# A fixed table of numbers instead of a greedy list sets the order of 1874 operations (input projection, convolution and attention) and of the 235 after them

## The chip, the cores and the metric

The kernel runs on one core of one Trainium2 chip. The time of a run is the device time of one launch in microseconds (us). Before the change three runs took 1118.74 us in the median (1118.23, 1118.74 and 1120.79). Lower is better. A core has a matmul engine (PE, TensorE, with its weight loads in a lane of their own, PEld), a vector engine (DVE), a scalar engine (ACT), a general engine (POOL, GpSimd) and a sync engine (SP) that here only issues DMAs. Each works through its own instructions strictly in the order in which they were written.

## The reference

One layer of a decoder: 1024 tokens, width 1024, float32.

```python
h = rms_norm(x, norm1_g)
q, k, v, glu_a, glu_b = split(h @ w_in)          # five times 512 columns
q, k = rms_norm(q per head), rms_norm(k per head) # 8 heads of 64
# stick-breaking attention, strictly causal, in blocks of 128 queries:
z = q @ k.T / 8;  beta = sigmoid(z)
A[t, s] = beta[t, s] * prod(1 - beta[t, j] for s < j < t);  attn = A @ v
c = glu_a * sigmoid(glu_b)
c = silu(layer_norm(causal_depthwise_conv(c, width 31)))
x = x + concat([attn, c]) @ w_out
h = rms_norm(x, norm2_g);  gate, val = split(h @ w_up)   # two times 2816 columns
x = x + (silu(causal_depthwise_conv(gate, width 3)) * val) @ w_down
```

## The kernel before

**Precision.** Every large product is made in three matmuls of a 512-column tile (`mm3`, L325 to L327): each operand is split into a high half, which the PE takes at its fast rate, and the low half that is left over, and high times high, low times high and high times low are added up in one PSUM bank. So each operand costs a rounding copy (the "high", mostly on ACT) and a subtraction (the "low", mostly on DVE, which reads what ACT wrote).

**Stages, in order of time.** (1) 0 to 40 us: the eight 128-token tiles of x are loaded (`load_x`, L422), squared on ACT (L431), given 1/rms on POOL (L316, L317), scaled on DVE (L435), turned by the PE (`hT`, L444) and split (L448 ACT, L449 DVE). The weights come in pieces (L475), are split (L479 ACT, L483 DVE), and the first products for v begin. The small parameters come as one operation of ten DMAs (`params`, L842 to L877, DMAs L850 to L855). (2) 40 to 236 us: the projections on the PE, and beside them the convolution on DVE, ACT and POOL. (3) 236 to 429.5 us: attention, head by head, with the last part of the convolution and the convolution's half of the output projection (`op`, L1353 its sum) put in between. (4) 429.5 to about 500 us: the attention's half of the output projection (`opa`, L1484 its sum), the second norm, and the turning of its result (`h2T`). (5) to 905 us the wide FFN products, (6) to the end the last product (`dn`, L1848).

**Attention.** For one head and one block of 128 queries (`tb`): the PE makes the scores in one or two pieces (`z`, L1172 and L1173), ACT makes 1 - beta of them (`nb`, L1180), DVE runs the products along the row as a scan (L1194), POOL or ACT takes one off the result (`less`, L1199 on POOL, L1201 on ACT). Two such blocks make a group g (0 to 3). The PE turns the group's weights (`wT`, L1221: `wT7_3_2` is head 7, group 3, source pair 2), they are split (high: ACT L1232, or DVE; L1230 for the triangle on the diagonal; low: DVE L1242, diagonal L1237), and the PE multiplies them with v into `po` (L1249). Two groups share one `po` bank, which ACT (L1277) and DVE (L1280) then fetch into `attn`. Keys and queries of a head are split and turned before (L1076 to L1136). DVE thus stands twice in the chain of each block, in the scan and in the low half.

**The end of attention.** Four pieces of 128 rows of w_out's attention half (`rawo`) are loaded into two places (L1387), split into `hio` (ACT, L1391) and `loo` (DVE, L1396), and `opa` takes them in the order of rows 0, 1, 3, 2.

**What sets the order.** All the work up to the end of attention is not emitted as it is written but collected in a `Plan`: 1874 operations, each with its engine or its alternatives (`{"ACT": 600, "DVE": 690}`, a cost in ns), the operations it comes after, the buffer places that it takes, and a key, which is about its due time. `Plan.run` (L124 to L204) is a list scheduler: at each step it looks at the operations that are ready and whose key is at most `HORIZON` above the lowest key open, works out for each the engine on which it would end first, and emits the one that could start first, where an operation that stands next by its key is given 150 ns (`PATIENCE`) of advantage. A second plan of 235 operations does the same for stage 4 and the first operands of stage 5. Afterwards `in_order` (L401) chains the emitted instructions of PE, DVE, ACT and POOL, so that each engine takes them in the order of emission. Stages 5 and 6 lie outside the plans.

## Time and profile before

| | |
|---|---|
| three runs | 1118.23, 1118.74, 1120.79 us |
| profiled execution | its time is its span, 1118.1 us |
| TensorE clock, mean share granted | 1.00 from 40 us on |
| PE | 1094.5 us busy, 98% of the span |
| DVE, ACT, POOL | 884.7, 618.6, 546.6 us |
| bytes moved | 118.5 MB, mean 106 GB/s |

A row of a timeline gives start, duration, engine, line of the code, operation and "out<-in" by the names of the tiles, then in brackets the idle time just before it and what ended that. A row of waits gives the waiting engine and line, the one waited for, the total in us, how often, and the longest. A row of a table of windows gives the stretch, its length, then busy time and instructions of PE, PEld, DVE, ACT and POOL, the granted clock, the DMAs' busy share and GB/s. A row of groups gives line, engine, operation, tiles, shapes and count, then busy us and mean ns of one, then the idle time in front of them. For PE a matmul's row lasts longer than the distance to the next one (0.39 us and 0.23 us for 512 columns), since matmuls are pipelined.

### The profile page before, as it was taken

Reading aid. Unit: us, or ns where it says so; the run is one execution under the profiler, and the core shown is the slowest. Engines: PE = TensorE matmul, PEld = TensorE weight load, DVE = VectorE, ACT = ScalarE, POOL = GpSimd, SP = SyncE. Lnnn points to the kernel's source line nnn. Section 1 sums busy time; section 2 is a strip of 40 time slices with the busy share of each in tenths; the row PEclk is TensorE's granted clock in tenths of the full one; section 3 lists DMA queues with packets and bytes.
Section 4 is the critical chain, followed back from the end, with each engine's and each line's share of the span. In section 5 each row is a group of like instructions: output and inputs, shape, how many; then the busy total and the mean of one; then the engine's idle time right before and its main releaser. Section 6 shows DMA issues by size and latency. Waiting matters only on the chain.

```text
span 1118.1 us, 14908 instructions
## 1 busy us (share of the span) xinstructions
PE 1094.5 (98%) x5255; PEld 906.2 (81%) x5255; DVE 884.7 (79%) x1188; ACT 618.6 (55%) x1137; POOL 546.6 (49%) x485
## 2 busy tenths in 40 slices
PE   8999999989999999989999999999999999999998
PEld 5888888768888887868888888888888888888887
DVE  6498899579998886889886777777777668787895
ACT  7344567787887674654443433333333378776760
POOL 3165587566344432656332233223323189887770
PEclk9999999999999999999999999999999999999999
DMA  8110500333933224442232231312222482303304
GB/s 286 57 39 8 143 20 24 95 128 88 282 121 113 58 76 151 154 147 76 94 93 96 73 97 59 107 62 97 73 95 76 141 323 83 143 14 146 151 2 150
DMA packets 110234, 118.54 MB, mean 106 GB/s; under 512 B 21105, under 2 KB 89936, under 8 KB 110158
## 3 DMA queue, kind: packets, MB, share of 16 engines
q1 hardware_dynamic: 110014, 117.05, 32.1%
q8 instruction: 42, 0.69, 0.3%
q10 hardware_dynamic: 144, 0.52, 0.1%
q14 instruction: 34, 0.28, 0.1%
HBM read 82.95 MB, written 28.31 MB: 100 GB/s over the span
## 4 chain that ended last, share of the span: by engine, by line
PE 77%; DVE 9%; POOL 4%; ACT 4%; DMA 2%; issue 2%; SPq 0%; POOLq 0%; DVEq 0%; ACTq 0%
PE dn L1848 19%; PE u_S L326 7%; PE u_S L327 7%; PE u_S L325 7%; PE u L327 5%; PE u L326 5%; PE u L325 5%; POOL attn L725 3%; PE po L1249 2%; PE wT L1221 2%; DVE nb L1194 2%; PE opa L325 1%; PE opa L327 1%; PE opa L326 1%; PE z L1172 1%
## 5 line engine op out<-in xcount | busy, mean ns | idle before, releaser
L1848 PE MATMUL dn<-wd,wd 128*128 128x512 f32 x768 | 181.5, 389 | 0.0
L1848 PEld LDWEIGHTS dn<-wd,wd 128*128 128x128 f32 x768 | 144.0, 188 | 30.1 <-DVE c L1851 0.2
L326 PE MATMUL u_S<-bT,aS 128*128 128x512 f32 x264 | 102.8, 389 | 0.8 <-DVE bT L1523 0.8
L327 PE MATMUL u_S<-bT,aS 128*128 128x512 f32 x264 | 102.7, 389 | 0.0
L325 PE MATMUL u_S<-bT,aS 128*128 128x512 f32 x264 | 102.5, 390 | 0.0
L1851 DVE TENSOR_TENSOR c<-dn,c 128x512 f32<-128x512 f32 x120 | 81.0, 684 | 23.9 <-PE dn L1848 23.7
L321 ACT CAST aS<-rawu 128x512 fp32r<-128x512 f32 x63 | 38.9, 621 | 96.2 <-PE u_S L327 66.9
L1753 ACT CAST wd<-rawd 128x512 fp32r<-128x512 f32 x128 | 72.6, 618 | 32.7 <-DMA rawd<-in_w_down_dram 10.8
L1194 DVE TENSOR_TENSOR_SCAN nb<-nb,one 128x128 f32<-128x128 f32 (+4 forms) x64 | 84.8, 1340 | 2.9 <-ACT nb L1180 2.7
L1595 POOL TENSOR_TENSOR s<-rawu 128x512 f32<-128x512 f32 x21 | 29.7, 1415 | 101.7 <-DMA rawu<-in_w_up_dram 92.5
L1752 ACT COPY whole<-rawd 128x512 f32<-128x512 f32 x110 | 63.4, 585 | 24.3 <-DVE wd L1754 11.2
L1754 DVE TENSOR_TENSOR wd<-whole,wd 128x512 fp32r<-128x512 f32 x90 | 59.9, 683 | 16.5 <-ACT wd L1753 9.4
L1601 POOL TENSOR_TENSOR rawu<-rawu 128x512 f32<-128x512 f32 x21 | 29.0, 1381 | 81.2 <-DVE a L322 81.2
L1697 DVE SCALAR_TENSOR_TENSOR y<-gv,cols_a,y 128x1023 f32<-128x1023 f32 (+1 forms) x44 | 59.6, 1355 | 10.2 <-ACT y L1695 10.2
L321 ACT CAST a<-rawu 128x512 fp32r<-128x512 f32 x63 | 39.0, 621 | 49.9 <-PE u_S L327 31.1
L325 PE MATMUL u<-b,a 128*128 128x512 f32 x168 | 65.5, 390 | 0.0
L327 PE MATMUL u<-b,a 128*128 128x512 f32 x168 | 65.5, 390 | 0.0
L326 PE MATMUL u<-b,a 128*128 128x512 f32 x168 | 65.4, 389 | 0.0
L326 PEld LDWEIGHTS u_S<-bT,aS 128*128 128x128 f32 x264 | 49.6, 188 | 11.4 <-POOL raws L1560 1.2
L325 PEld LDWEIGHTS u_S<-bT,aS 128*128 128x128 f32 x264 | 49.5, 188 | 10.7 <-ACT bT L1522 0.4
L327 PEld LDWEIGHTS u_S<-bT,aS 128*128 128x128 f32 x264 | 49.6, 188 | 10.3
L322 DVE TENSOR_TENSOR a<-rawu,a 128x512 fp32r<-128x512 f32 x63 | 47.0, 748 | 13.2 <-ACT a L321 13.2
(343 smaller groups left out, 3213.6 us busy)
## 6 DMA issues: line engine op xcount, KB each, us to landing
rawu<-in_w_up_dram SPq DMA_DIRECT2D x44, 512.0 KB
act_d<-y SPq DMA_DIRECT2D x22, 512.0 KB
rawd<-act_d SPq DMA_DIRECT2D x22, 512.0 KB
rawd<-in_w_down_dram SPq DMA_DIRECT2D x22, 512.0 KB
raw_qk<-in_w_in_dram SPq DMA_DIRECT2D x16, 256.0 KB
rawo<-in_w_out_dram SPq DMA_DIRECT2D x8, 512.0 KB
m<-conv_d SPq DMA_DIRECT2D x16, 256.0 KB
xt<-in_x_dram SPq DMA_DIRECT2D x8, 512.0 KB
```

The source lines that it names most:

```text
L321: nc.scalar.copy(hi, src)
L322: lo_engine.tensor_tensor(lo, src, f32(hi), op=ALU.subtract)
L325: nc.tensor.matmul(ps, a_hi, b_hi, start=first, stop=False)
L326: nc.tensor.matmul(ps, a_hi, b_lo, start=False, stop=False)
L327: nc.tensor.matmul(ps, a_lo, b_hi, start=False, stop=last)
L1194: nc.vector.tensor_tensor_scan(rev, rev, ones_of[0][:, :w], 0.0, op0=ALU.mult, op1=ALU.max)
L1697: nc.vector.scalar_tensor_tensor(y[:, j:], g[:, :S - j], par("fw", (KF - 1 - j) * NF + f), y[:, j:], op0=ALU.mult, op1=ALU.add)
L1752: nc.scalar.copy(whole, src)
L1753: nc.scalar.copy(t[:, 0], src)
L1754: lo_engine.tensor_tensor(t[:, 1], whole, f32(t[:, 0]), op=ALU.subtract)
L1848: nc.tensor.matmul(ps, a[:, tok], b, start=first and m == 0, stop=last and m == 2, skip_group_check=True)
L1851: nc.vector.tensor_tensor(sums[c][s], ps, sums[c][s], op=ALU.add)
```

## The change

`Plan.run` no longer chooses. It is given a list of numbers and emits the operations in that order: 1874 numbers for the first plan and 235 for the second. `HORIZON` and `PATIENCE` go. What it still works out as it walks through the list is on which of its alternative engines an operation runs and which buffer place it gets; that goes by costs, and these are changed: hand-over times by engine, a time for PE's results to come out, a time for PE to start again after a pause, and some thirty operations' own costs (most by less than a third). Two dependencies are added: the keys' split of every head but the first also waits for the last use of the weights whose room it takes, and the first `po` product of an odd group waits for the last of the even one. No operation is added or taken away, and nothing changes outside the two plans.

```diff
-    HAND_OVER, POOL_HAND_OVER = 60, 130
+    HAND_OVER = {"ACT": 36, "DVE": 36, "POOL": 86, "PE": 56, "SP": 30}
+    OVER = {"PE": 0, "ACT": 104, "DVE": 82, "POOL": 36, "SP": 0}
+    PE_DRAIN, PE_RESTART = 163, 100
...
-    def run(self, busy):
+    def run(self, order):
...
-            for op in ready:
-                if op.key > horizon:
-                    continue
...
-                rank = (max(start - PATIENCE, at[e]), op.key) if op.key <= main[low].key + 1 else (start, op.key)
+        for op in (self.ops[n] for n in order):
+            slots = self.slots_for(op.takes)
...
+                    r = max(r, o.end + (0 if o.engine == e == "PE" else Plan.HAND_OVER[e] + (Plan.PE_DRAIN if o.engine == "PE" else 0)))
+                start = max(r, at[e])
+                if e == "PE" and start > at[e] + 30:
+                    cost += Plan.PE_RESTART
...
-        k2 = split_op("k", staged, 0, base - (2.6 if h else EARLY), ready, khl)
+        k2 = split_op("k", staged, 0, base - (2.6 if h else EARLY), ready + (second_used if h else []), khl)
...
-                b = add({"POOL": 100 + 1.03 * w, "ACT": 160 + 0.86 * w}, less, i - AHEAD_SCAN + 0.3 * u, [a])
+                b = add({"POOL": 192 + 0.84 * w, "ACT": 296 + 0.84 * w}, less, i - AHEAD_SCAN + 0.3 * u, [a])
...
-                last = add("PE", 480, products, k, [c] + v2 + ([last] if last else []))
+                last = add("PE", 480, products, k, [c] + v2 + ([last] if last else [prev_last] if g % 2 else []))
...
-    plan.run({})
+    plan.run(ORDERS[0])
...
-    plan.run({})
+    plan.run(ORDERS[1])
```

The first places of the two lists:

```diff
+ORDERS = [[int(n) for n in numbers.split()] for numbers in ("""
+0 13 32 1 25 33 41 34 35 42 2 4 43 95 15 38 7 47 36 37 26 5 3 44 39 104 45 105 48 59 60 22 24 6 46 106 49 113 68 114
```

Lines past L260 have numbers higher by 60 in the changed kernel (L1194 becomes L1254); the text keeps the numbers of before.

**DVE at the start of attention.** Before the change, these rows stand on DVE from the first scan (L1194) on; `conv_lo` (L820) is the last of the convolution, `nb0_0` to `nb0_3` are rows of head 0, and `rest<-qT` (L1136) is the low half of its queries.

```order
L1194 SCALAR_TENSOR_TENSOR nb0_0_2204<-nb0_0_2204,one_1898 128x128
L1194 SCALAR_TENSOR_TENSOR nb0_2_2215<-nb0_2_2215,one_1898 128x384
L820 TENSOR_TENSOR conv_lo1_0_2230<-conv_out0_812,conv_hi1_0_2229 128x512
L1136 SCALAR_TENSOR_TENSOR rest_2170<-qT0_1_2239,qgain_130,keys_2148 128x512
L820 TENSOR_TENSOR conv_lo1_0_2230<-conv_out1_1087,conv_hi1_0_2229 128x512
L1194 SCALAR_TENSOR_TENSOR nb0_1_2249<-nb0_1_2249,one_1898 128x256
L1194 SCALAR_TENSOR_TENSOR nb0_3_2266<-nb0_3_2266,one_1898 128x512
L1230 CAST diagonal_0_1752<-wT0_0_0_2275 128x384
```

After the change, the same place on DVE:

```order
L1196 SCALAR_TENSOR_TENSOR rest_2198<-qT0_0_2187,qgain_130,keys_2154 128x512
L880 TENSOR_TENSOR conv_lo1_0_2223<-conv_out0_878,conv_hi1_0_2222 128x512
L1254 SCALAR_TENSOR_TENSOR nb0_2_2230<-nb0_2_2230,one_2184 128x384
L1196 SCALAR_TENSOR_TENSOR rest_2198<-qT0_1_2236,qgain_130,keys_2154 128x512
L1254 SCALAR_TENSOR_TENSOR nb0_0_2227<-nb0_0_2227,one_2184 128x128
L1159 CAST keys_2154<-kT1_0_2217 128x512
L1254 SCALAR_TENSOR_TENSOR nb0_1_2269<-nb0_1_2269,one_2184 128x256
L1196 SCALAR_TENSOR_TENSOR rest_2198<-qT1_0_2263,qgain_130,keys_2154 128x512
L880 TENSOR_TENSOR conv_lo1_0_2223<-conv_out1_1176,conv_hi1_0_2222 128x512
L1290 CAST diagonal_0_1825<-wT0_0_0_2301 128x384
```

The queries' low halves, those of head 1 among them, and a copy of head 1's keys have come in between the first scans, so that a scan stands after other work that does not need it.

**DVE at the end of attention.** Before, from the low half of `wT7_3_0` to the last fetch of `po` (`attn`, L1280):

```order
L1396 TENSOR_TENSOR loo2_4300<-rawo_4165,hio2_4299 128x1024
L1242 TENSOR_TENSOR tl_2344<-wT7_3_0_4330,rest_2170 128x512
L1242 TENSOR_TENSOR tl_2344<-wT7_3_1_4336,rest_2170 128x512
L1232 CAST rest_2170<-wT7_3_2_4342 128x512
L1242 TENSOR_TENSOR tl_2344<-wT7_3_2_4342,rest_2170 128x512
L1237 TENSOR_TENSOR diagonal_1_2985<-wT7_3_3_4349,diagonal_1_2985 128x384
L1396 TENSOR_TENSOR loo3_4376<-rawo_4165,hio3_4375 128x1024
L1280 TENSOR_TENSOR attn_110<-po7_2_4269,attn_110 64x512
```

After, the same place on DVE:

```order
L1302 TENSOR_TENSOR tl_2407<-wT7_3_0_4325,rest_2198 128x512
L1302 TENSOR_TENSOR tl_2407<-wT7_3_1_4315,rest_2198 128x512
L1456 TENSOR_TENSOR loo0_4341<-rawo_3825,hio0_4340 128x1024
L1302 TENSOR_TENSOR tl_2407<-wT7_3_2_4355,rest_2198 128x512
L1297 TENSOR_TENSOR diagonal_1_3067<-wT7_3_3_4343,diagonal_1_3067 128x384
L1456 TENSOR_TENSOR loo3_4373<-rawo_3825,hio3_4372 128x1024
L1340 TENSOR_TENSOR attn_110<-po7_2_4276,attn_110 64x512
L1456 TENSOR_TENSOR loo1_4396<-rawo_3825,hio1_4395 128x1024
```

The low half of w_out's second piece (`loo1`), which `opa` takes second, now stands behind the fetch of the last `po`, and on ACT its high half (`hio1`) stands behind that fetch in the same way; before, both pieces 0 and 1 were made well ahead.

**SP at the opening.** Before, the tiles of x are all issued ahead of the parameters (`param_rows`):

```order
L422 DMA x_q0_139<-in_x_dram 128x1024
L422 DMA x_qk1_140<-in_x_dram 128x1024 x4
L475 DMA raw_glu_b0_246<-in_w_in_dram 128x8x128
L850 DMA param_rows_272<-in_conv_dw_b_dram 4x128
L850 DMA param_rows_272<-in_conv_ln_g_dram 4x128
```

After, the same queue:

```order
L535 DMA raw_v_2_237<-in_w_in_dram 128x2x256 x2
L910 DMA param_rows_247<-in_conv_dw_b_dram 4x128
L910 DMA param_rows_247<-in_conv_ln_g_dram 4x128
L910 DMA param_rows_247<-in_conv_ln_b_dram 4x128
L910 DMA param_rows_247<-in_ffn_dw_b_dram 22x128
L913 DMA param_rows_247<-in_q_norm_g_dram 1x64 x2
L913 DMA param_rows_247<-in_k_norm_g_dram 1x64 x2
L914 DMA param_rows_247<-in_ffn_dw_w_dram 66x128
L915 DMA param_rows_247<-in_conv_dw_w_dram 124x128
L482 DMA x_qk1_140<-in_x_dram 128x1024 x3
L482 DMA x_q0_139<-in_x_dram 128x1024
```

The ten parameter loads now stand ahead of four of the eight tiles of x and of the last piece of v's weights.

128 lines of the change are left out of this document (50 added, 78 removed), and 80 rows, old and new, of the table ORDERS.

## The prediction

> **What bounds the kernel now.** I read the page's first line, then a table of windows cut at the stages (the columns: stretch, length, busy us of PE, PEld, DVE, ACT and POOL with their instructions, clock, DMA share, GB/s).
>
> ```profile
> span 1118.1 us, 14908 instructions
> ```
>
> ```profile
> 0.00:40.00 40.00, 34.58 (x164) 25.44 (x164) 26.91 (x38) 25.36 (x44) 13.04 (x24) 0.96 0.69 226
> 40.00:235.70 195.70, 194.74 (x893) 159.78 (x891) 156.68 (x219) 111.97 (x253) 117.25 (x114) 1.00 0.20 59
> 235.70:317.30 81.60, 75.66 (x475) 64.62 (x473) 76.06 (x98) 66.67 (x131) 42.19 (x45) 1.00 0.55 165
> 317.30:429.50 112.20, 108.36 (x704) 94.10 (x704) 97.80 (x118) 82.75 (x157) 43.57 (x46) 1.00 0.28 89
> 429.50:500.00 70.50, 66.80 (x321) 54.04 (x320) 56.19 (x87) 40.77 (x80) 36.48 (x41) 1.00 0.48 159
> 500.00:904.90 404.90, 404.90 (x1788) 335.31 (x1787) 302.31 (x366) 154.81 (x223) 139.66 (x96) 1.00 0.30 97
> ```
>
> PE is the bound. An order can win only the time in which PE waits inside the planned part, and none after 500 us, where PE is never idle and the plans no longer rule. Idle PE (length less the first busy figure) is 5.42, 0.96, 5.94, 3.84 and 3.70 us in the first five rows.
>
> That is not yet all that is lost, as a matmul's row overlaps the next:
>
> ```profile
> 452.97 0.39 PE L327 MATMUL opa<-hio,m 128*128 128x512 f32 x1
> 453.89 0.47 PE L325 MATMUL opa<-hio,m 128*128 128x512 f32 x1 [0.54 <-DVE x L1484]
> 454.20 0.40 PE L326 MATMUL opa<-loo,m 128*128 128x512 f32 x1
> ```
>
> Matmuls of this form start 0.23 us apart when nothing is late. Here the starts lie 0.92 apart, so 0.69 is lost where the bracket shows 0.54, and the next start comes 0.08 late again (0.31 for 0.23). So I took in the trace every distance between two starts of PE, less the usual one of its form, and added them up: 6.2 us up to 40, 2.3 to 235.7, 10.7 to 317.3 (26 stops), 8.8 to 429.5 (35 stops), 5.5 to 500. The first and the last of these 61 stops in attention:
>
> ```profile
> 241.58 0.45 PE L1172 MATMUL z<-keys 128*128 128x384 f32 x1 [1.05 <-ACT nb L1180]
> ...
> 428.57 0.38 PE L1249 MATMUL po<-tl,rest 128*128 128x256 f32 x1 [0.41 <-DVE tl L1242]
> ```
>
> What PE waits for most in attention, then what DVE itself waits for in the first stretch, and in the second (total, times, longest):
>
> ```profile
> PE z L1172 <- ACT nb L1180: 3.4, 6, 1.1
> PE po L1249 <- DVE tl L1242: 1.4, 3, 0.8
> PE wT L1221 <- DVE tl L1242: 1.4, 2, 0.8
> ```
>
> ```profile
> DVE nb L1194 <- ACT nb L1180: 2.6, 4, 1.1
> DVE rest L1136 <- ACT keys L1133: 1.4, 1, 1.4
> ```
>
> ```profile
> DVE tl L1242 <- ACT rest L1232: 6.3, 7, 2.1
> DVE diagonal L1237 <- ACT diagonal L1230: 2.5, 4, 1.2
> ```
>
> Two different pictures. In the first stretch DVE is busy 76.06 us of 81.60, more than PE: both are near full, and DVE's 5.5 idle us are lost to its order. In the second DVE has 14.4 us to spare, PE 3.8: there the stops are a matter of distance, of how much PE work stands between what PE makes and what it needs back.
>
> **The change part by part.**
>
> *PE's work* stays the same, instruction for instruction; only its order differs. The stages after 500 us have nearly the same rows: nothing.
>
> *Opening.* Ten parameter loads pass ahead of four tiles of x on SP:
>
> ```profile
> 14.30 3.67 SPq L850 DMA_DIRECT2D param_rows<-in_conv_dw_b_dram  x1
> ...
> 24.99 0.25 SPq L855 DMA_DIRECT2D param_rows<-in_conv_dw_w_dram  x1
> ```
>
> In the trace of before these ten took from 14.30 to 25.24, 10.9 us, behind all the loads of x and of v's weights; the last, with nothing left ahead of it, took 0.25. Ten of those are 2.5 us. In the new order they stand early, while the DMAs still have the loads ahead of them to move, so the tiles behind them can be issued before the DMAs run dry. I take 0; −2 if the earlier weights help (PE's 5.42 idle us are all ahead of 25 us), +5 if half of the 10.9 us comes back.
>
> *Projections:* 2.3 us are lost, of which I let 1.0 go, as PE's rows alternate between two products there now; 0 to −2.
>
> *First attention stretch.* On DVE, from the first scan to the low half of head 2's third group, 96 rows become 91. Gone from DVE are three diagonal copies, one rest copy, one keys copy and one `conv_lo`, and one scan of 640 more has come in:
>
> ```profile
> L1194 DVE TENSOR_TENSOR_SCAN nb<-nb,one 128x640 f32<-128x640 f32 x4 | 5.9, 1476 | 0.4 <-ACT nb L1180 0.4
> ...
> L820 DVE TENSOR_TENSOR conv_lo<-conv_out,conv_hi 128x512 fp32r<-128x512 f32 x4 | 3.9, 974 | 0.4 <-ACT conv_hi L809 0.3
> ...
> L1230 DVE CAST diagonal<-wT 128x384 fp32r<-128x384 f32 x4 | 2.2, 543 | 0.0
> ...
> L1232 DVE CAST rest<-wT 128x512 fp32r<-128x512 f32 x2 | 1.4, 684 | 0.1
> L1099 DVE CAST keys<-kT 128x512 fp32r<-128x512 f32 x2 | 1.3, 672 | 0.0
> ```
>
> 3 x 0.543 + 0.684 + 0.672 + 0.974 − 1.476 is 2.5; as a `conv_lo` that meets nothing takes 0.69 (its row below), 0.3 of that is doubtful, and I take 2.2. DVE's work is then 73.9 us. Its idle 5.5 I put at 3.0, since in the new rows other work stands between the first scans, so that `nb` has time to come: 76.9 in place of 81.6, −4.7. PE does 69.0 us of work there in place of 70.0, so 1.0 comes later: −3.7. Bounds: DVE's work alone and no better filling, −2.2 + 1.0 = −1.2; all of its idle gone, −7.7 + 1.0 = −6.7.
>
> *Second stretch.* Here I counted the PE work between the turning of weights (`wT`) and the `po` that needs them: the median goes from 1.85 to 2.69 us, and of 80 such distances 18 were below 1.6 us and 2 are now. Within that distance must fit a copy on ACT and a low half on DVE, of some 0.6 and 0.7 (the copies 0.58 and 0.684 in this part's rows are of that size), and the ways between, so 1.6 was short: nearly all of the `po` and `wT` stops should go, of the `z` stops (whose distances are unchanged) not all. 8.8 lost becomes 3.0: −5.8; bounds −3 (no more than the 2.8 in the two rows of `tl`) and −8.8.
>
> *A new wait at the end.* `loo1` is made behind the last fetch of `po`. Rows of before:
>
> ```profile
> 427.10 1.05 ACT L1391 CAST hio<-rawo 128x1024 fp32r<-128x1024 f32 x1
> ...
> 428.90 1.22 DVE L1396 TENSOR_TENSOR loo<-rawo,hio 128x1024 fp32r<-128x1024 f32 x1
> ...
> 429.71 0.58 ACT L1277 COPY attn<-po 64x512 f32<-64x512 f32 x1 [1.55 <-PE po L1249]
> ```
>
> After the last `po`: fetch 0.58, `hio1` 1.05, `loo1` 1.22, with the ways between some 3.0; PE has three matmuls of piece 0 and one of piece 1 to do, 4 x 0.23. That leaves about +2.3 (1.2 if the ways cost nothing and ACT is ahead, 4 if the fourth `rawo`, which needs a place that `loo0` frees, lands late). Behind it wait all the later `opa`.
>
> *Stage 4:* PE's rows are the same, its 5.5 stay: 0.
>
> *One engine moved:* 22 of the `less` go from ACT to POOL:
>
> ```profile
> L1199 POOL TENSOR_SCALAR nb<-nb 128x640 f32<-128x640 f32 x6 | 4.8, 800 | 2.8 <-DVE nb L1194 2.8
> ```
>
> At 0.80 that is 17.6 us of work for an engine that is busy 42.19 + 43.57 = 85.8 of 193.8 us here: hidden by POOL's own idle time. What it costs DVE is the question. One `conv_lo` that met POOL took over twice what another took:
>
> ```profile
> 242.07 0.69 DVE L820 TENSOR_TENSOR conv_lo<-conv_out,conv_hi 128x512 fp32r<-128x512 f32 x1
> ...
> 249.39 1.73 DVE L820 TENSOR_TENSOR conv_lo<-conv_out,conv_hi 128x512 fp32r<-128x512 f32 x1
> ```
>
> The scans, though, all take the same, 1476 for 640 columns with POOL at work beside some of them. So I count 0. [...]
>
> **Sum:** 0 − 1.0 − 3.7 − 5.8 + 2.3 + 0 = −8.2. The profiled execution's span is 1118.1, 0.6 under the median of three runs, 1118.74. So 1109.9, and 1110.5 as a median.
>
> **The rivals.**
>
> *Nearly every wait in the planned part goes:* each term at its good end, −2.0 in the projections, −6.7 and −8.8 in attention and a new wait of 1.2, makes −16.3, a median of 1102.4. For: PE has the same work in fewer places where it must wait for DVE. Against: DVE is 73.9 of 76.9 us full in the first stretch even by my own count, and the `z` distances did not grow. Chance 0.17.
>
> *The opening pays.* Tiles of x arrive 5 us late: 1115.5 (1113.5 to 1118). For: the ten loads did take 10.9 us. Against: each alone takes 0.25, and other work can be done first. Chance 0.16.
>
> *Nothing changes.* DVE's work is nearly what it was, and each stop that is removed comes back at the next shortage of DVE: 1118. Against it: distances, not DVE, make the second stretch's stops. Chance 0.08.
>
> *Slower: POOL's added work holds DVE.* If `less` on POOL blocks DVE for its own length, 17.6 us come back on an engine that is 93% full in the first stretch (76.06 of 81.60): −8.2 + 17.6 is +9.4, about 1128. From 8.2 of the 17.6 on, 47% of it, the kernel is slower. Against: the even scan rows. Chance 0.05.
>
> **How the numbers follow.** My own forecast (1106 to 1113.5, from the bounds of the two stretches) has 0.54. A measurement tells about 0.2% here, 2.2 us. Faster by more: 0.54 + 0.17 + 0.11 of the opening's case (to 1116.5): 0.82. Same: 0.05 + 0.07 of no change: 0.12. Slower: 0.05 + 0.01: 0.06. The range 1103 to 1117 leaves out part of the first rival, and most of the last two, some 0.2.
>
> **What would show it.** Windows of the changed kernel cut at the same operations: first attention stretch about 78 us in place of 81.6 with DVE idle about 3; in the second, stops of `po` and `wT` behind `tl` gone; one stop of 2 us or more at the first `opa`, behind `loo1`; `hT` on time before 25 us. I am wrong if PE's waits keep their sum under other names, if PE idles over 7 us before 40, if scans exceed 1476 for 640 columns, or if the gain lies after 500 us.

## The result: 0.7% slower, and the profile after

The changed kernel took 1128.05 us in the median of four runs (1127.47 to 1128.72), before 1119.34 beside it: a ratio of 1.0070, 95% interval 1.0055 to 1.0084. It is 8.7 us slower where 8.2 faster was predicted. The profiled execution's span is 1125.9 us in place of 1118.1.

The same table of windows as in the prediction, of the changed kernel, cut at the same places of the program:

```profile
span 1125.9 us, 14908 instructions
```

```profile
0.00:40.00 40.00, 30.93 (x140) 22.96 (x141) 24.66 (x27) 22.45 (x38) 17.53 (x27) 0.91 0.69 226
40.00:241.10 201.10, 198.79 (x916) 163.16 (x916) 156.79 (x221) 119.63 (x279) 119.54 (x114) 1.00 0.18 56
241.10:321.00 79.90, 72.60 (x464) 62.08 (x463) 74.41 (x90) 60.21 (x129) 49.35 (x56) 1.00 0.54 164
321.00:428.40 107.40, 107.40 (x713) 95.68 (x712) 97.17 (x118) 75.36 (x147) 52.40 (x58) 1.00 0.28 87
428.40:510.00 81.60, 72.77 (x330) 58.48 (x329) 60.67 (x89) 42.34 (x82) 39.68 (x43) 0.94 0.46 154
```

In the fourth row PE is never idle by its rows: there the table does what it was made for. All the other rows pay for it. Up to 40 us PE is idle for 9.07 us (before 5.42), more than the 7 that the prediction named as a sign of being wrong, and in the first and the fifth row the granted clock is below 1.

PE's work now stands in another order, so equal times are not equal places. I therefore took at some marks the time at which PE starts the first matmul of a tile, less the work of all matmuls ahead of it at their usual distances. This *lag* is what PE has lost up to there, to waits and clock together (us, worked out from each kernel's trace; e6 to e18 are experiments told below; opa0_0, opa0_1 and opa4_0 are the first three tiles of `opa`, and the row opa4 is the start of the third):

```
                         before  after    e6     e9    e12    e18
first v                    7.9    10.2    8.0    7.8    7.8    7.8
first kT (attention)      13.8    18.3   16.2   14.5   12.5   13.3
wT2_3_3 (1st stretch)     25.5    31.1   28.1   26.3   24.3   25.1
first opa (2nd stretch)   35.6    34.4   40.3   36.3   29.4   30.1
opa4                      35.6    41.4   40.4   36.3   33.6   31.4
opa7_1 (end of stage 4)   36.5    42.3   41.5   37.3   37.4   32.4
span                    1118.1  1125.9 1125.6 1118.3 1118.6 1113.4
```

So after against before: +2.3 up to the first v, +2.3 in the rest of the projections, +1.0 in the first stretch of attention, −6.7 in the second, +6.9 at the first two tiles of `opa`, −0.1 in the rest of stage 4, and +2.1 behind it: +7.8. The first v starts at 15.6 us; cut at 40 us, where the prediction cuts, the opening pays 2.9 and the rest of the projections 1.7.

**The opening.** DVE, POOL and PE at 8 to 14 us:

```profile
8.46 1.28 DVE L495 SCALAR_TENSOR_TENSOR x_k<-x_k,rs,attn 128x1024 f32<-128x1024 f32 x1 [6.70 <-POOL rs L377]
...
10.41 2.35 POOL L543 TENSOR_TENSOR lo_v<-raw_v,hi_v 128x1024 fp32r<-128x1024 f32 x1
10.45 3.39 DVE L495 SCALAR_TENSOR_TENSOR x_k<-x_k,rs,attn 128x1024 f32<-128x1024 f32 x1 [0.71 <-POOL rs L377]
...
13.99 1.94 PE L504 MATMUL hT<-ident_r,x_k 128*128 128x128 f32 x8 [3.10 <-DVE x_k L495]
```

The low half of v's first weights, which was DVE's before, is now on POOL, and DVE's scaling of the second tile, 1.28 us by itself, takes 3.39 beside it: it ends 1.08 after POOL does (10.41 + 2.35 = 12.76, 10.45 + 3.39 = 13.84). PE waits 3.10 for it. Before, the scaling of that tile ended later still (13.62 + 1.28 = 14.90), but PE had products of v to do in the meantime. The ten parameter loads stand on SP in the meantime, here the first, the last and the tiles of x behind them:

```profile
8.51 0.33 SPq L910 DMA_DIRECT2D param_rows<-in_conv_dw_b_dram  x1
...
15.36 0.30 SPq L915 DMA_DIRECT2D param_rows<-in_conv_dw_w_dram  x1
15.70 1.31 SPq L482 DMA_DIRECT2D x_qk<-in_x_dram  x3
```

Those tiles are issued 7.2 us behind the first parameter, and the DMAs run dry ahead of them: in the microseconds from 14 and from 15 their share is 0.04 and 0.02, before 1.03 and 1.04.

**The end of attention**, SP, ACT, POOL, DVE and PE together:

```profile
427.87 1.84 POOL L1413 TENSOR_TENSOR xt<-prod,xt 128x512 f32<-128x512 f32 x1 [7.19 <-ACT prod L1410]
...
429.70 1.04 ACT L1451 CAST hio<-rawo 128x1024 fp32r<-128x1024 f32 x1 [0.54 <-DMA rawo<-in_w_out_dram]
429.74 0.32 SPq L1420 DMA_DIRECT2D x_part<-xt  x1
430.80 0.50 PE L385 MATMUL opa<-hio,m 128*128 128x512 f32 x1 [1.56 <-ACT hio L1451]
430.85 3.95 SPq L1516 DMA_DIRECT2D x<-x_part  x3
432.75 1.22 DVE L1456 TENSOR_TENSOR loo<-rawo,hio 128x1024 fp32r<-128x1024 f32 x1 [2.86 <-DMA x_part<-xt]
...
434.02 0.80 PE L386 MATMUL opa<-loo,m 128*128 128x512 f32 x1 [2.72 <-DVE loo L1456]
434.62 0.63 PE L387 MATMUL opa<-hio,m 128*128 128x512 f32 x1
435.05 0.63 PE L385 MATMUL opa<-hio,m 128*128 128x512 f32 x1
```

`loo1` does not start when `hio1` is done at 430.74, but at 432.75, when a store has landed: its place in the buffers is that of `xt`, the last token tile's sum of the convolution half, whose other half (op7_0) the table puts behind op7_1, at the very end. The plan's list of that store's predecessors names only the sum of op7_1. So the plan has the store landed before the sum of op7_0 is made, and the place free as soon as that sum ends; the 3.0 us from the store's issue to the start of `loo1` (429.74 to 432.75) are missing in it. `hio1` itself waits last for its load, 0.54 us on ACT behind the fetch of `po`. PE loses 1.56 and 2.72 us, and then the matmuls start 0.43 us apart (434.62, 435.05) where 0.23 is usual.

**The clock.** Windows of the changed kernel around the three falls (clock is the figure behind POOL's):

```profile
12.00:18.50 6.50, 4.51 (x15) 3.96 (x16) 4.86 (x5) 3.77 (x7) 1.00 (x3) 0.50 0.56 186
...
431.00:439.00 8.00, 5.28 (x14) 3.93 (x14) 4.01 (x6) 0.71 (x2) 0.00 (x0) 0.57 0.87 305
...
488.00:494.00 6.00, 5.13 (x14) 3.87 (x15) 4.70 (x8) 4.47 (x10) 2.46 (x5) 0.72 0.39 111
```

The clock stands at half for whole windows of 3.41 us: one in before's trace, from 13.9 us, five here, two from 11.8, two from 431.6 and one from 489.6 (the last 5 us left out in both). At half clock, a window in which PE works throughout costs half its length, 1.71 us, one in which it also waits costs less: of the 6.83 us from 431.6 on PE's rows are idle for 2.4, so the clock costs some 2.2 there, half of the other 4.4. The falls lie on an even grid, 123 and 17 such windows apart. In the window just ahead of these three PE's rows are idle for 2.3, 1.9 and 2.0 us, never for all of it.

The other traces bear this out. From 20 us to 3 us ahead of PE's end all of them together have 37 windows at full clock that are followed by a fall, and PE's rows are idle in these for 1.57 to 2.91 us. Every window with more than 1.70 us of idle time was followed by a fall, none with less than 1.57 was (in the first 10 us three with 1.73 to 1.90 kept the clock, and before's fall at 13.9 came behind 1.55). So about half a window of idle time, in one stop or in several, could be enough in these runs, and it mattered where the grid cut a stop: the changed kernel's stop of 2.48 us ahead of 255.38 lies across two windows, with 1.21 and 1.57 us of idle time, and the clock stayed at 1.

### The profile page after: what moved, and what is told of

Same layout as the page of the kernel before. It is cut to its first block, busy times and chain, and to the rows that moved or that the text cites. A ratio compares the mean times of both kernels' runs of the same rounds, so it can differ in the third digit from the quotient of the medians.

```text
span 1125.9 us, 14908 instructions
## 1 busy us (share of the span) xinstructions
PE 1094.7 (97%) x5255; PEld 909.1 (81%) x5255; DVE 886.5 (79%) x1174; ACT 610.4 (54%) x1144; POOL 569.7 (51%) x511
## 4 chain that ended last, share of the span: by engine, by line
PE 79%; DVE 6%; POOL 5%; DMA 4%; ACT 3%; issue 2%; SPq 0%; DVEq 0%; POOLq 0%; ACTq 0%
PE dn L1908 19%; PE u_S L387 7%; PE u_S L386 7%; PE u_S L385 7%; PE u L387 5%; PE u L386 5%; PE u L385 5%; POOL attn L785 3%; PE po L1309 3%; PE wT L1281 2%; DVE conv_a L758 2%; PE z L1232 1%; PE z L1233 1%; PE op L385 1%; PE op L387 1%
## 5 line engine op out<-in xcount | busy, mean ns | idle before, releaser
L1254 DVE TENSOR_TENSOR_SCAN nb<-nb,one 128x640 f32<-128x640 f32 (+7 forms) x64 | 84.7, 1339 | 2.1 <-ACT nb L1240 1.9
L1814 DVE TENSOR_TENSOR wd<-whole,wd 128x512 fp32r<-128x512 f32 x90 | 59.8, 684 | 15.6 <-ACT wd L1813 8.6
L1259 POOL TENSOR_SCALAR nb<-nb 128x384 f32<-128x384 f32 (+7 forms) x55 | 39.3, 720 | 49.6 <-DVE nb L1254 48.0
L386 PEld LDWEIGHTS u_S<-bT,aS 128*128 128x128 f32 x264 | 49.6, 188 | 10.3
L385 PEld LDWEIGHTS u_S<-bT,aS 128*128 128x128 f32 x264 | 49.6, 188 | 10.3
```

What stands on the lines that cost most here:

```text
L385: nc.tensor.matmul(ps, a_hi, b_hi, start=first, stop=False)
L386: nc.tensor.matmul(ps, a_hi, b_lo, start=False, stop=False)
L1254: nc.vector.tensor_tensor_scan(rev, rev, ones_of[0][:, :w], 0.0, op0=ALU.mult, op1=ALU.max)
L1814: lo_engine.tensor_tensor(t[:, 1], whole, f32(t[:, 0]), op=ALU.subtract)
```

## The experiments

Each ratio is against the kernel before, run beside it on the same chip, whose medians lay between 1119.10 and 1120.30 us. Operations are named by their numbers in the table; 26 is the ten parameter loads. The second list has 237 numbers, 0 to 236, and not 235.

**e1: the first 128 operations in before's order.**

```diff
-0 13 32 1 25 33 41 34 35 42 2 4 43 95 15 38 7 47 36 37 26 5 3 44 39 104 45 105 48 59 60 22 24 6 46 106 49 113 68 114
...
+0 1 4 13 7 14 10 15 22 32 23 33 2 34 24 5 3 35 25 41 38 6 16 36 42 39 37 8 19 40 104 50 43 105 26 106 11 9 51 44 47 45
...
```

> The first 128 operations (the opening, until all eight tiles of x are split) stand in the order of before, all the others in the order of the table. Theory A (the change loses in two places that lie outside attention, the opening and the first opa, and wins inside attention): the opening's 4.6 us come back, about 1123.5 us, and the lag at the first scores falls from 18.6 to about 14. Rival B (DVE's total work sets the end of attention, so what the opening gains is waited for later): within 1.5 us of 1128. Rival C (the gain is more than the opening's, as half the clock's drop goes too and the later projections run better): below 1121.

Measured 1125.61, 1.0052 (1.0037 to 1.0067); span 1123.4. The lag at the first kT is 15.0 in place of 18.3, and 39.2 in place of 42.3 at opa7_1. The opening's order costs some 3 us by the profile, 0.6 of it at the clock, which falls for one window there in place of two; by the times alone it is not told from the table, whose interval meets this one. The rest of the loss stays.

**e2: the table, but the ten parameter loads, with the turns and the copy that need them, behind v's last weights.**

```diff
-0 13 32 1 25 33 41 34 35 42 2 4 43 95 15 38 7 47 36 37 26 5 3 44 39 104 45 105 48 59 60 22 24 6 46 106 49 113 68 114
+0 13 32 1 25 33 41 34 35 42 2 4 43 95 15 38 7 47 36 37 5 3 44 39 104 45 105 48 59 60 22 24 6 46 106 49 113 68 114 96
+115 23 14 61 8 116 86 9 65 107 40 87 117 50 62 88 63 51 64 52 10 26 108 109 11 12 16 19 69 17 70 18 66 20 244 118 131
...
```

> Of the table only the ten parameter loads (and the two turns on PE that need them, with a copy on DVE) are moved: behind the tiles of x and the last piece of v's weights. Theory A1 (the DMAs ran dry between 12 and 15 us because SP was busy with the ten): the gap in the DMAs is gone, the fifth tile of x is squared 3 us earlier, and PE saves 2 to 3 us: 1125.5. Rival A2 (the opening is lost on DVE, whose scaling of the second tile took 3.39 us beside POOL, and PE is behind before the fifth tile matters): no more than 0.7 us, 1127.5.

Measured 1126.09, 1.0058 (1.0043 to 1.0073). First v at a lag of 7.9, as before the change, first kT at 15.7. By the times alone it is not told from the table (its interval meets the table's); by the lag at the first kT the loads are worth 2.7 of the opening's loss, with the same 0.6 of clock in it. The DMAs' share at 14 and 15 us is 1.03 and 1.01 again.

**e3: the table, but the low half of v's first weights held on DVE, right behind the scaling of the second tile.** Of the edit the choice of engine:

```diff
-        b = add({"DVE": 1215, "POOL": 2450}, lambda eng: (nc.vector if eng == "DVE" else nc.gpsimd).tensor_tensor(
+        b = add({"DVE": 1215} if name == "v_0" else {"DVE": 1215, "POOL": 2450}, lambda eng: (nc.vector if eng == "DVE" else nc.gpsimd).tensor_tensor(
```

> Of the table only the low half of the first piece of v's weights goes from POOL to DVE, right behind the scaling of the second tile of x. Theory A2 (POOL's subtraction holds DVE's scaling, both with two operands in SBUF): the scaling takes 1.28 us instead of 3.39, the second turn comes at 11.9 us instead of 14.0, PE's clock falls less, and 2 to 3 us are saved: 1125.5. Rival A1 (the late loads decide): the first products start earlier but PE then waits for the same late weights, below 0.7 us: 1127.5.

Measured 1130.07, 1.0090 (1.0073 to 1.0107). No gain: the scaling takes 1.28, but with this order of DVE `h_lo` is late instead (2.9 us of waits of `hT`), and the clock falls for one window from 13.9 and one from 34.4 us, where the table has two from 11.8. The stretched `x_k` alone does not explain the opening.

**e4: the end of the table: the pieces 1 and 2 of w_out exchanged, op7_0's last steps and its store together.**

```diff
-1712 1713 1717 1849 1698 1850 1863 1724 1714 1718 1699 1725 1864 1720 1715 1721 1851 1722 1852 1872 1726 1719 1873
...
-1853 1723 1854 1727 1861 1728 1865 1866 1729 1867
+1698 1850 1851 1852 1853 1854 1861 1863 1724 1714 1718 1699 1725 1864 1720 1715 1721 1722 1872 1726 1719 1873 1723
+1727 1728 1868 1869 1729 1870
```

> Of the table only its last part is changed: the second and the third piece of w_out change places (the one that opa takes last is now made last), and the last half tile of op, its fetch, its sum and its store stand as early as their bank allows. Theory A (the low half of the piece waited for the place that the store of this half tile frees, 2.89 us of DMA behind a late sum): the stop at the first opa falls from 4.7 us to 1 or 2, the clock doesn't fall behind it, and 4 to 6 us are saved: 1123. Rival D (the wait is for the load of the fourth piece, which is as late as before): 1.4 us at most, 1126.7.

Measured 1127.37 (1125.94 to 1132.77), 1.0078 (1.0050 to 1.0106). Inconclusive by time: the profiled execution, the slowest of the four (1132.77), lost the clock for one more window in the opening (from 34.2) and for two from 259.5. In it the stops at `opa` shrink to 1.0 (`hio`) and 0.8 (`loo`), a `po` stop of 1.1 has come in, and from wT7_3_3 to opa7_1 the lag grows by 6.7 instead of 8.0.

**e5: the table, and the first two `opa` tiles take w_out's piece 1 last.**

```diff
-                for kk in range(4):
-                    mm3(d["ps", nn], d["m"][:, 0, kk, :], d["m"][:, 1, kk, :], w_attn[ROWS[kk]][0][:, cols], w_attn[ROWS[kk]][1][:, cols], kk == 0, kk == 3)
+                steps = [(nn, kk) for kk in range(4)] if t else [(nn, 0), (nn, 3), (nn, 2)] + ([(0, 1), (1, 1)] if nn else [])
+                for n, kk in steps:
+                    cs = slice(n * 512, (n + 1) * 512)
+                    mm3(d["ps", n], d["m"][:, 0, kk, :], d["m"][:, 1, kk, :], w_attn[ROWS[kk]][0][:, cs], w_attn[ROWS[kk]][1][:, cs], kk == 0, kk == (3 if t else 1))
```

> The table as it is, but the first two tiles of opa share the late piece of w_out: three pieces for the first, three for the second, then the late one for both. So 18 matmuls (4.1 us) stand between the end of attention and the first use of the late piece, in place of 3. Theory A: PE then waits 1 to 1.5 us at one place in place of 4.3 at two, the clock stays up, and 4.5 to 6 us are saved: 1122.5 to 1123.5. Rival E (what is won there is waited for later, since the norm behind opa or its loads are late anyway): at most 1.5 us, 1126.5 or more.

Measured 1129.56 (1125.96 to 1130.44), 1.0078 (1.0064 to 1.0092). From the first `opa` to opa4 the lag grows by 3.5 instead of 6.9, but from there to opa7_1 by 2.6 instead of 0.9: `opa` waits 1.9 for the sum `x`, which needs x loaded from `x_part`. Half of what one stop gives comes back in the next, another 1.1 is lost behind opa7_1, where the clock falls for two windows in place of one, and the time is no better than the table's.

**e6: before's order under the new rules and costs.**

```diff
-0 13 32 1 25 33 41 34 35 42 2 4 43 95 15 38 7 47 36 37 26 5 3 44 39 104 45 105 48 59 60 22 24 6 46 106 49 113 68 114
...
+0 1 4 13 7 14 10 15 22 32 23 33 2 34 24 5 3 35 25 41 38 6 16 36 42 39 37 8 19 40 104 50 43 105 26 106 11 9 51 44 47 45
...
```

> The order of before, written as a table, under the changed rules: only the choice of engine and of buffer place, and the two added dependencies, differ from before. Theory A (the order itself made the loss): within 2 us of before, 1118 to 1121. Rival F (the choice of engine made it: more work on POOL, which holds DVE): 1124 or more.

Measured 1128.48 (1127.80 to 1129.14), 1.0074 (1.0061 to 1.0087). With the old order this is as slow as the table. So something besides the order costs 8 us there: what the new costs choose, or the added dependencies. The planner puts 42 operations on other engines than before.

**e7 and e8: before's order up to operation 1300 of its list, the table's behind it; e8 with e5's split too.** The first line is e6's, the last ones are the table's:

```diff
+0 1 4 13 7 14 10 15 22 32 23 33 2 34 24 5 3 35 25 41 38 6 16 36 42 39 37 8 19 40 104 50 43 105 26 106 11 9 51 44 47 45
...
+1850 1863 1724 1714 1718 1699 1725 1864 1720 1715 1721 1851 1722 1852 1872 1726 1719 1873 1853 1723 1854 1727 1861
+1728 1865 1866 1729 1867
```

> The first 1300 operations (to the last weights of the third head, about 315 us) in the order of before, the other 574 in the order of the table, its end among them. Theory A (the table wins 6.6 us in the second part of attention and loses 6.3 at its end and about 2 behind it): the lag at the first opa is about 29 us, 6 less than before, the end gives it all back, 1118 to 1122. Rival G (the table's second part is only good behind its own first part): the lag there is 33 or more, 1124 or more.

> The last one, with the first two tiles of opa sharing the late piece as above. Theory A: the gain of the second part of attention stays, less 1.3 us: 1112.5 to 1115, the fastest of all. Rival E (the end of attention's gain is waited for later): 1118 or more.

Measured 1128.25, 1.0075 (1.0062 to 1.0088), and 1127.47, 1.0063 (1.0047 to 1.0078). In e7 the lag grows by 4.9 in the second stretch (before 10.0), and by 7.9 from the first `opa` to opa7_1: the table's gain and its loss are both in its last third, and e8 keeps 1.4 more.

**e9: e6, with all 289 operations that have a choice held on before's engines.** The first lines of the list, and its use:

```diff
+FORCED = {(237, 5): "DVE", (237, 7): "DVE", (237, 19): "ACT", (237, 20): "DVE", (237, 27): "DVE", (237, 29): "DVE",
...
-            for e, cost in op.cost.items():
+            for e, cost in [(k, c) for k, c in op.cost.items() if FORCED.get((len(self.ops), op.n), k) == k]:
```

> The order of before as a table, and every operation that has alternatives held to the engine that it had before; only the choice of buffer places and the two added dependencies are left of the change. Theory H (the choice of engine under the new costs makes most of what the order of before lost under the new rules): back to 1119 to 1121.5. Rival I (the buffer places or the two dependencies made it): 1125 or more.

Measured 1120.06 (1118.15 to 1120.57), 1.0005 (0.9996 to 1.0014). The 8 us are gone. The added dependencies and the way of emission are in e9 as in e6. The buffer places are not all the same: they are given out by planned times, so 71 operations have another place in e6 (in `s`, `nb` and `o`), while in e9 the planner gives every operation the engine and the place that it had before. So on before's order it is the choice of engines, with the places that follow from it. Of the 7.3 us between the two profiles some 3 are the clock's: in e6 it falls for one window at 246.8 and one at 502.8, in e9 for none there.

**e10: e9, with the 20 `less` that the new costs move to POOL there.**

```diff
-          1096): "ACT", (1874, 1104): "ACT", (1874, 1110): "ACT", (1874, 1112): "ACT", (1874, 1116): "ACT", (1874,
+          1096): "ACT", (1874, 1104): "POOL", (1874, 1110): "POOL", (1874, 1112): "ACT", (1874, 1116): "ACT", (1874,
...
```

> The last one, but the 20 operations that take one off the scan's result are on POOL in place of ACT, as the new costs choose. Rival J (POOL's added work holds DVE, the fourth rival of the prediction): 5 us or more over the last one. Theory H' (the scans read one operand from PSUM and are not held; these 20 are hidden by POOL's idle time, and the cost lies in the few other moves): within 2 us of the last one.

Measured 1119.70, 1.0009 (1.0000 to 1.0017): not it, on this order. `less` on POOL does not hold the scans; those of 640 columns take 1478 ns in the changed kernel, 1476 before.

**e11: the table, with two operations of the second plan held on before's engines.**

```diff
+FORCED = {(237, 227): "POOL", (237, 232): "DVE"}
```

> The changed kernel, with two operations of the second plan held to their engines of before: the difference of two up-projection blocks on POOL again, the sum beside it on DVE. Theory K (these two make the stop of 1.7 us at the first FFN products, which is new in every kernel built from the changed one, and help the clock fall there): 2 to 3.5 us less, 1124.5 to 1126. Rival L (that stop and the clock's fall have to do with when stage 4 ends, not with these): within 1 us of 1128.

Measured 1126.20 (1124.98 to 1129.45), 1.0071 (1.0057 to 1.0084). Its ratio is that of the table, so by time nothing is shown. In the profile opa7_1 has the table's lag (41.7, 42.3) and the span is 2.7 less, 2.2 of it behind opa7_1.

**e12: before's order and engines up to operation 1300, the table behind it, before's engines in the second plan, and e5's split.** The edit is e9's list of engines without the later operations, on e8.

```diff
+FORCED = {(237, 5): "DVE", (237, 7): "DVE", (237, 19): "ACT", (237, 20): "DVE", (237, 27): "DVE", (237, 29): "DVE",
...
-                for kk in range(4):
...
+                steps = [(nn, kk) for kk in range(4)] if t else [(nn, 0), (nn, 3), (nn, 2)] + ([(0, 1), (1, 1)] if nn else [])
...
```

> The first 1300 operations in the order and on the engines of before, the other 574 in the order of the table, the second plan on its engines of before, and the late piece of w_out last for the first two tiles of opa. Theory A with H: the gain of the second part of attention (5 us of waits) stays, the end gives 2 to 4 of it back: 1115 to 1118, faster than both. Rival E: the end and what follows give all of it back: 1119 or more.

Measured 1121.14 (1119.30 to 1121.77), 1.0016 (1.0007 to 1.0025). The first `opa` starts 6.2 us ahead of before (lag 29.4 against 35.6), and opa7_1 0.9 behind it. Against e8, which has the same order, only engines (of 22 operations) and the places that follow differ: 1.0016 in place of 1.0063, so the engines cost some 5 us here too. Its end of attention, all engines:

```profile
424.69 0.32 SPq L1458 DMA_DIRECT2D x_part<-xt  x1
...
425.87 4.08 SPq L1554 DMA_DIRECT2D x<-x_part  x3
...
427.90 1.22 DVE L1494 TENSOR_TENSOR loo<-rawo,hio 128x1024 fp32r<-128x1024 f32 x1 [3.05 <-DMA x_part<-xt]
...
429.18 0.50 PE L424 MATMUL opa<-loo,m 128*128 128x512 f32 x1 [1.33 <-DVE loo L1494]
...
432.19 0.69 DVE L1584 TENSOR_TENSOR x<-opa,x 128x512 f32<-128x512 f32 x1 [1.72 <-DMA x<-x_part]
...
433.02 0.77 PE L423 MATMUL opa<-hio,m 128*128 128x512 f32 x1 [2.41 <-DVE x L1584]
```

Everything hangs on the store of `xt` at 424.69: `loo1` takes its room, and x is loaded behind it. Two stops, 1.33 and 2.41, and the clock is at half for two windows, 431.9 to 438.8.

**e14: e12 with op7_0 and that store earlier in the order.**

```diff
-1705 1692 1831 1665 1668 1690 1693 1696 1669 1694 1691 1860 1711 1670 1697 1716 1671 1695 1712 1713 1717 1849 1698
-1850 1863 1724 1714 1718 1699 1725 1864 1720 1715 1721 1851 1722 1852 1872 1726 1719 1873 1853 1723 1854 1727 1861
+1705 1692 1831 1665 1668 1690 1693 1696 1669 1694 1691 1860 1711 1670 1697 1716 1671 1849 1850 1695 1712 1851 1852
+1713 1717 1853 1854 1861 1698 1863 1724 1714 1718 1699 1725 1864 1720 1715 1721 1722 1872 1726 1719 1873 1723 1727
```

> Edit: as in e12 (before's order and engines up to operation 1300, the table behind it, the second plan on before's engines, the first two opa tiles taking w_out's second piece last), and the last token tile's second sum of the convolution half (op7_0, its fetch, its sum, its store) put some 2.7 us of PE work earlier. Theory S (in e12 the time won in the second half was lost because x of stage 4 is loaded only behind the last store of xt, and loo1 takes that tile's room): the last x_part store at 422 or earlier in place of 424.7, no wait of loo1, no wait of the first sum x, no half clock at 431 to 439; opa 2 us later than in e12 but the end 3 to 6 us earlier: 1115 to 1118. Rival C (the stops only move to wT and po of the last group, and the clock falls all the same): 1120 to 1122.

Measured 1119.84, 1.0002 (0.9992 to 1.0012). A miss as a test: op7_0 must wait for its PSUM bank (PE waits 0.8 for DVE's `attn`), and the store goes out at 425.32, no earlier. The first `opa` is 4.6 us later than in e12; the clock does not fall, and the end is the same.

**e15, e16, e17: e9, with one group of moved operations each on the engines of the new costs.** e15 the second plan's pair, e16 twelve copies of attention, e17 the eight operations ahead of attention; of the last two the first lines:

```diff
-          "DVE", (237, 225): "DVE", (237, 227): "POOL", (237, 229): "POOL", (237, 231): "DVE", (237, 232): "DVE",
+          "DVE", (237, 225): "DVE", (237, 227): "DVE", (237, 229): "POOL", (237, 231): "DVE", (237, 232): "POOL",
```

```diff
-          1160): "POOL", (1874, 1162): "DVE", (1874, 1166): "DVE", (1874, 1180): "ACT", (1874, 1186): "ACT", (1874,
+          1160): "POOL", (1874, 1162): "ACT", (1874, 1166): "ACT", (1874, 1180): "ACT", (1874, 1186): "ACT", (1874,
...
```

```diff
-          "DVE", (1874, 21): "DVE", (1874, 112): "ACT", (1874, 121): "ACT", (1874, 130): "ACT", (1874, 139): "DVE",
+          "DVE", (1874, 21): "DVE", (1874, 112): "ACT", (1874, 121): "ACT", (1874, 130): "ACT", (1874, 139): "ACT",
...
```

> Edit: as e9 (before's order, before's engines, the new rules for the rest), but the two operations of the second plan, the low half of S2 of the second a block and a sum, on the engines that the new costs choose. Theory H2 (this pair makes the stops at the start of the FFN): 2 to 4 us over e9's 1120.06, so 1122 to 1124, with u0_S1 late and nothing changed ahead of opa7. Rival: under 0.7 us, and the loss of before's order under the new costs is made elsewhere.

> Edit: as e9, but the twelve copies of attention that the new costs place otherwise (turned weights, diagonals, keys: five from ACT to DVE, six from DVE to ACT, one from POOL to ACT) go where the new costs place them. Theory H3 (these copies make PE wait in attention): 3 to 5 us over e9, so 1123 to 1125, with po and wT stops behind ACT or DVE in the second stretch. Rival (the plan's own costs are right here: they give PE's end 1.7 us earlier): 1118 to 1120.

> Edit: as e9, but the eight operations ahead of attention that the new costs place otherwise (two fetches and one more of projections, two scales, one low half of a weight from DVE to POOL, the sums of the convolution from POOL to DVE, a high half from ACT to POOL) go where the new costs place them. Theory H4 (the opening of projections pays): 1.5 to 2.5 us over e9, so 1121.5 to 1122.5, lost ahead of the first kT. Rival: under 0.7 us. If e15, e16 and e17 together do not make 8 us over e9, the parts are not additive and what is left is the clock or the meeting of several moves.

Measured 1121.92, 1.0019 (1.0010 to 1.0029); 1121.11, 1.0017 (1.0007 to 1.0026); 1123.50, 1.0032 (1.0021 to 1.0043). Over e9's 1.0005 that is 0.0014, 0.0012 and 0.0027, and with e10's 0.0004 together 0.0057 of e6's 0.0069 (6.4 of 7.7 us): no single move, but three groups, nearly additive within their intervals (those of e15 and e16 meet e9's, so singly only e17 is told from it). In e15 and e10 no buffer place differs from e9's; in e16 49 do, in e17 22. Each is lost where its group works: e17's lag is 17.3 at the first kT (e9 14.5), e16's grows by 11.9 in the second stretch (e9 10.0), e15's is 35.7 at opa7_1, below e9's 37.3, and its loss, 1.4 by the profile, comes behind that (the profiled execution, 1119.88, is the fastest of its ten and has no fall of the clock in the opening).

e15 shows how an exchange of engines costs. In e9 (DVE and POOL, start of the FFN), where DVE has the sums and one of the low halves `aS`, and POOL two of these:

```profile
492.19 0.68 DVE L1767 TENSOR_TENSOR aS<-s,aS 128x512 fp32r<-128x512 f32 x1
...
493.00 2.56 POOL L1767 TENSOR_TENSOR aS<-rawu,aS 128x512 fp32r<-128x512 f32 x2 [3.69 <-ACT aS L1763]
```

In e15, where one of POOL's two went to DVE and the last sum (`rawu`) from DVE to POOL, and the PE behind them:

```profile
490.15 1.62 POOL L1767 TENSOR_TENSOR aS<-rawu,aS 128x512 fp32r<-128x512 f32 x1 [2.49 <-ACT aS L1763]
490.54 1.78 DVE L1767 TENSOR_TENSOR aS<-s,aS 128x512 fp32r<-128x512 f32 x1
...
491.73 1.75 POOL L1774 TENSOR_TENSOR rawu<-rawu 128x512 f32<-128x512 f32 x1
...
492.25 1.78 DVE L1767 TENSOR_TENSOR aS<-rawu,aS 128x512 fp32r<-128x512 f32 x1
...
497.08 0.50 PE L445 MATMUL u<-b,a 128*128 128x512 f32 x1 [2.46 <-DVE a L440]
```

DVE's 0.68 becomes 1.78 twice: each time it ends 0.55 behind POOL (491.77 and 492.32; 493.48 and 494.03), as if it stood still until POOL was through. The low half of `a`, five rows further on DVE, comes late, and PE waits 2.46. `x_k`'s row in the opening ended 1.08 behind POOL's, the same picture at twice the width.

In e17, what PE waits for between 40 and 236 us (columns: total, times, longest), its first two rows:

```profile
PE ln L879 <- DVE conv_out L858: 1.0, 1, 1.0
PE qk L443 <- ACT hi_qk L597: 0.9, 1, 0.9
```

In e9 neither stands, and its longest wait there is 0.6. DVE, which has got the convolution's sums, is behind: its row of `lo_qk` at 183.3 us in e9 comes at 184.8. Which of the eight does most was not taken apart.

**e18: e12 with one sum left out, that of op7_0 into `xt`, and the store behind the other sum. e19: the same in the table.** Half a row of the last token tile then lacks the convolution's share; PE's, DVE's and ACT's instructions stay, POOL has one of 1.8 us less.

```diff
-                def summed(nn=nn, d=d, cols=cols):
-                    nc.gpsimd.tensor_tensor(d["x"][:, cols], d["prod", nn], d["x"][:, cols], op=ALU.add)
+                def summed(nn=nn, d=d, cols=cols, t=t):
+                    if (t, nn) != (7, 0):
+                        nc.gpsimd.tensor_tensor(d["x"][:, cols], d["prod", nn], d["x"][:, cols], op=ALU.add)
```

> Edit: e12, and one sum left out, that of op7_0 into xt (the convolution's share of half a row of the last token tile is thus missing from the result), so that xt's store can go behind the other sum, some 13 us earlier; PE's, DVE's and ACT's instructions stay. Theory S (what e12 wins up to the first opa is given back because that late store holds loo1's room and stage 4's loads of x): no wait of loo1 for x_part, x loaded before the first sum, no stops at opa, no half clock at 431 to 439, opa7 4 to 6 us ahead of before: 1113 to 1116. Rival (other work, DVE's or ACT's, is next in line at once): 1119 to 1121.

> Edit: the changed kernel with the same sum left out and the store behind the other sum (the same part of the result is missing). Theory S: loo1 waits for hio1 alone, the stop at the first opa falls from 2.7 to 1 or less and the lag that grows by 6.3 us within the first opa grows by 2 or less: 1122 to 1125. Rival (the stop is made by loo1's place behind the last fetch of po, as the prediction had it): 1127 to 1128.

Measured 1116.10, 0.9969 (0.9957 to 0.9980), and 1125.75, 1.0059 (1.0043 to 1.0076). e18's end of attention, to be held against e12's:

```profile
411.35 4.31 SPq L1459 DMA_DIRECT2D x_part<-xt  x2
...
424.30 4.48 SPq L1555 DMA_DIRECT2D x<-x_part  x3
...
426.72 1.22 DVE L1495 TENSOR_TENSOR loo<-rawo,hio 128x1024 fp32r<-128x1024 f32 x1 [1.15 <-ACT hio L1490]
...
429.97 0.69 DVE L1585 TENSOR_TENSOR x<-opa,x 128x512 f32<-128x512 f32 x1 [0.69 <-DMA x<-x_part]
```

`loo1` follows `hio1`, the first sum `x` comes 2.2 us earlier, PE's longest stop there is 1.1 in place of 2.41, and the clock stays at 1. The lag from the first `opa` to opa7_1 grows by 2.3 in place of 8.0. That in e12 the late store gives the gain of the second part back is shown. In the table itself it is a part: in e19 the stop behind `loo` falls from 2.7 to 0.8, that behind `hio` stays (1.7, the table 1.56), the clock falls for one window there in place of two, and up to opa4 the lag grows by 4.4 in place of 6.9. By time e19 is not told from the table, and it missed the 1122 to 1125 expected.

No kernel here that computes everything beats the kernel before: e9, e10 and e14 equal it, e12 is 0.16% behind.

## Why the prediction was wrong

Three terms of the sum failed most: the new wait at the end (+2.3, measured +6.9), the first stretch (−3.7, measured +1.0), and the engines, put at 0, whose share the experiments show on two other orders.

*Second stretch, −5.8.* Right: −6.7, with PE never idle. The stops of `po` and `wT` are gone, as the longer distances between them would have it; e7 and e12 show the gain with only that part of the table, but no run changed the distances alone.

*The new wait, +2.3.* Right in place, wrong in size and partly in cause: +6.9. I counted the work on ACT and DVE behind the last `po` and not the room that `loo1` takes. That room is held by a store that the table had moved to the end, and which I had not followed, though the prediction itself names `rawo`'s place as a way to be late. What I had counted is there: without the late store e19 has stops of 1.7 and 0.8, 2.5 in all. With it they are 1.56 and 2.72, 4.6 by the distances of the starts, and the clock adds some 2.2, a term that no part of the sum had. e19 and e18 show the store's share, the windows the clock's.

*The engines, 0.* I priced the moved `less` alone, found them free, which e10 confirms on before's order, and took the other rows of DVE, ACT and POOL for moved in time only. In the changed kernel the planner puts 76 operations on another engine than before. e6 and e9 show that on before's order the choice of engines under the new costs, with the buffer places that follow, is worth 8 us, e8 and e12 some 5 on another, and e15 to e17 that on before's order it is made of some twenty operations in three places. What happens in e15 is in its rows; for e16's copies and most of e17's operations the way in which they cost PE time was not taken apart. The stretch beside POOL, which the prediction saw in one `conv_lo` (1.73 in place of 0.69), is there in e15's pair too (1.78 in place of 0.68) and in `x_k` (3.39 in place of 1.28), where I did not look for it. How much of the table's own loss is choice, and how much order, stays open: before's engines under the table's order were not tried, since they were fitted to another order.

*Opening, 0; projections, −1.0.* +2.9 and +1.7. The step that failed is that the tiles could be issued before the DMAs run dry: they were issued 7.2 us behind the first parameter, and at 14 to 16 us the DMAs had next to nothing to move. The rival that the opening pays was right in kind: e1 takes back 3.3 of the 4.6 by its profile, e2 2.7, neither by its time. DVE stretched beside POOL is in the trace, but e3 shows that it is not by itself the cause.

*First stretch, −3.7.* +1.0. DVE's work did fall, to 74.41 us in 79.90, but its idle time stayed at 5.5. What PE waits for there, its first three rows:

```profile
PE z L1232 <- ACT nb L1240: 3.8, 4, 2.5
PE wT L1281 <- POOL nb L1259: 1.4, 2, 1.2
PE po L1309 <- DVE tl L1302: 1.3, 1, 1.3
```

The longest stop of the first row is of a new kind, ACT at 254 us:

```profile
254.53 0.62 ACT L869 CAST conv_hi<-conv_out 128x512 fp32r<-128x512 f32 x1 [2.45 <-DMA conv_d<-conv_lo]
...
255.38 0.50 PE L1232 MATMUL z<-keys 128*128 128x512 f32 x1 [2.48 <-ACT nb L1240]
```

A copy that waits for a store stands ahead of `nb` on ACT, and PE waits 2.48 for `nb`. Counting DVE's rows could not show that. The second row is `less` on POOL, which the prediction called hidden; its long stop is told in the last section. That DVE's idle time would fall to 3.0 was a choice, and it was wrong.

*After 500 us, nothing.* +2.1 behind opa7_1, one window of half clock from 489.6 among it. The pair of the second plan works there (e15), and with e11 the table's span loses 2.2 less behind opa7_1.

*The slower rival* had the right time, 1128, by the wrong mechanism: e10 excludes it on before's order, and in the changed kernel the scans are as fast as before (1478 ns for 640 columns, 1476 before).

## What to carry to other kernels

When a change of costs comes with a change of order, compare first which engine each operation runs on. Then put before's order under the new costs, and once more with before's engines: these two runs tell what the costs choose from what the order does. A gain in one stretch is only as good as the next thing that holds the stage behind it; follow the room of every buffer that the work at the seam takes, stores included. And where stops of PE add up to some 1.6 us within 3.41, which could be enough for a fall of the clock in these runs, a forecast should price that too: by half the length, up to 1.71 us for each window.

## What the runs showed of the hardware

- Stops can cost PE more than themselves: in after's end 4.3 us of stops go with some 2.2 us lost at half clock. In the traces of before and after every change of the clock lies on a grid of 3.41 us, and from 20 us on it fell, in all traces, behind windows with 1.57 us of idle time or more, not only behind wholly idle ones. The grid lay elsewhere in each execution (the fall in the opening starts at 13.90 in before's trace, at 11.46 in e9's, with the same order, engines and places, and lasts one window in the one and two in the other).
- DVE's rows with both inputs in SBUF that started beside a row of POOL already under way ended, in the places shown here, 0.55 us (128x512) or 1.08 us (128x1024) after POOL's end, whether they began 0.04 or 0.52 us behind POOL's start: as if DVE stood until POOL was through. A third place, in the first stretch of attention:

```profile
292.62 2.39 POOL L577 TENSOR_TENSOR v<-ahead,v 128x1024 f32<-128x1024 f32 x1
292.86 3.24 DVE L1367 TENSOR_TENSOR w_hl<-rawo,w_hh 128x1024 fp32r<-128x1024 f32 x1
```

POOL ends at 295.01, DVE at 296.10. In the next rows DVE started first, POOL's was the one that grew, and PE waited for it:

```profile
298.21 1.20 DVE L1367 TENSOR_TENSOR w_hl<-rawo,w_hh 128x1024 fp32r<-128x1024 f32 x1
298.45 1.43 POOL L1259 TENSOR_SCALAR nb<-nb 128x512 f32<-128x512 f32 x1 [3.44 <-DVE nb L1254]
...
299.94 0.55 PE L1281 MATMUL wT<-ident_r,nb 128*128 128x128 f32 x3 [1.18 <-POOL nb L1259]
```

The same DVE instruction takes 1.20, and the `less` beside it 1.43, where one of its size takes 0.74 in the mean; PE waits 1.18 for it. The scans were not held: 23 of the changed kernel's 64 ran beside a `less` on POOL, and of 640 columns all eight took 1459 to 1487 ns, four of them beside a `less`. So here a `less` on POOL did not hold DVE's scans, but a low half on DVE held the `less`. In e15 POOL's rows of 128x512 take 1.62 and 1.75 in place of 1.28 (half of 2.56); each starts while DVE's row ahead is still running.
- The rate at which PE takes the split operands: the starts of all three matmuls of a product lie 0.227 us apart for 512 columns, in the median of before's and of after's trace. That is what the part on precision calls the fast rate; no run has a product of unsplit operands beside it.
